# Two transformer blocks on one core: the weights of the layers done by halves lie 64 bytes further in their buffers

## The chip, the cores and the metric

The kernel runs on 1 core of one Trainium2 chip. The metric is the device time of one execution in microseconds (us); less is better. Before the change the median of three runs is 1825.68 us (1824.88 to 1826.26).

## What is computed

Two blocks, one after the other, on 512 tokens of 1024 features, in float32. Nearly all of the arithmetic is in dense layers `x @ w`. Cut to its layers, the reference is:

```
def first_block(x, ...):
    hn = rms_norm(x, g_mix_pre)
    proj = hn @ w_in                          # 1024 x 8192, in pieces
    br_a = spatial_gating(...) @ w_sgu_out
    br_b = conformer_conv(...) @ w_conv_out
    br_c = multiscale_pool(...) @ w_pool_out
    h = x + rms_norm(merged @ w_out, g_mix_post)
    f_gate, f_up = split(rms_norm(h, g_ffn_pre) @ w_ffn_in)
    h = h + rms_norm((silu(f_gate) * f_up) @ w_ffn_out, g_ffn_post)
    return h + sigmoid(h @ w_ple_gate) * (p @ w_ple)

def second_block(x, ...):
    proj = rmsnorm(x, norm_mix_w) @ w_in      # 1024 x 5640, in pieces
    oa = gated_delta_rule(...)                # 4 heads, chunks of 64
    ob = chunk_band_attention(...)            # 8 heads
    x = x + (gates on oa @ w_branch_a, ob @ w_branch_b) @ w_out
    u = causal_dwconv(rmsnorm(x) @ w_up) + conv_ffn_b
    x = x + (silu(gate) * up) @ w_down
    return rmsnorm(x, norm_final_w)
```

## The kernel before

Features lie on the 128 partitions, tokens run along a row, so an activation is 8 tiles of 128 x 512 and a layer's output block `n` (128 features) is summed in one PSUM bank over the input blocks `k`.

A float32 value is kept as two float32r tiles, `hi` (the value rounded) and `lo` (the rest). `mm3` then makes a product of three matmuls, `hi*hi`, `hi*lo` and `lo*hi`: lines 168, 169 and 170. The weight slice, 128 x 128, is the stationary operand that TensorE loads, and the activation is the moving one. Each matmul has a weight load of its own in the trace (LDWEIGHTS, engine PEld).

`prep` brings one chunk of weights, as a rule 128 x 1024, that is eight such slices: a DMA on SyncE's queue into `raw`, a copy on ScalarE into `whi` (line 113) and a subtraction on VectorE into `wlo` (line 116). Of `whi` and `wlo` there are four buffers each, 4096 bytes a partition. `emit` runs the list of steps in order and prepares chunks two ahead.

Most layers are done by `linear`: all 512 tokens at once, matmuls 512 columns wide. Five places are done by `linear_halves`: the same weights first for tokens 0 to 255, then for tokens 256 to 511, so that what follows can start on the first half. Its matmuls are 256 columns wide. These places are `w_out` (output blocks 4 to 7), `w_ffn_in` (the first two blocks), `w_ffn_out` (the last two), `w_ple_gate` (the first three) and `w_down_2` (the last two). Where `hold` gives other tiles for a chunk (named `fl`, `tl`, `xh`, `xl` by their pools), the weights are split into those and not into `whi` and `wlo`.

Every tile starts at a multiple of `LINE`, 128 bytes:

```
LINE = 128
...
        n = -taken % LINE
        if n:
            pool.tile([P, n // 4], F32, name="fill")
```

A slice of weights is 512 bytes of a partition's row, so every slice starts at such a multiple as well. `gm` holds masks of 128 x 128 for the delta rule; of its ten planes the kernel reads nine, 0 to 8 (`gm[:, 4 + lv]` with `lv` up to 4). The pool that holds it, `p2`, comes after the weight buffers, the activations and the small tiles in memory.

The order of the instructions is set by the code's order and, on VectorE within a short reach, by the recording layer's scheduler.

Of the kernel before, what the change touches and what calls it, by code (L numbers as in the profile page):

```python
# [8 lines left out]
F32 = mybir.dt.float32  # L9
F32R = mybir.dt.float32r  # L10
# [5 lines left out]
P = 128  # L16
T = 512
D = 1024
# [25 lines left out]
def build(tc, d, out):  # L44
# [13 lines left out]
    S = {}  # L58
# [87 lines left out]
            i = c.start // T  # L146
            return self.tiles[i][:, c.start - i * T:c.stop - i * T]

    def prep(src, hold=None):
        n = src.shape[-1]  # L150
        raw = wp.tile([P, D], F32, tag="raw", bufs=2, name="raw")
        nc.sync.dma_start(raw[:, :n], src)
        if hold is not None:
            hi, lo = [], []
            for c0 in range(0, n, T):
                h, l = hold(), hold()
                m = min(n - c0, T)
                split(raw[:, c0:c0 + m], h[:, :m], l[:, :m])
                hi.append(h)
                lo.append(l)  # L160
            return Parts(hi), Parts(lo)
        hi = wp.tile([P, D], F32R, tag="whi", bufs=4, name="whi")
        lo = wp.tile([P, D], F32R, tag="wlo", bufs=4, name="wlo")
        split(raw[:, :n], hi[:, :n], lo[:, :n])
        return hi, lo

# [73 lines left out]
    steps = []  # L240
    bgq = deque()

    def step(fn, chunk=None, bg=2400, hold=None):
        steps.append((chunk, fn, bg, hold))

    def emit():
        chunks = [(c, hold) for c, _, _, hold in steps if c is not None]
        pos = 0
        used = 0
        ready = deque()  # L250
        LA = 2
        for c, fn, bg, _ in steps:
            if c is not None:
                used += 1
                while pos < len(chunks) and pos < used + min(LA, used - 1):
                    ready.append(prep(*chunks[pos]))
                    pos += 1
                fn(*ready.popleft())
            else:
                fn()  # L260
            while bg > 0 and bgq:
                cost, f = bgq.popleft()
                f()
                bg -= cost
        assert not bgq
# [26 lines left out]
    def linear_halves(name, nbs, kb, xs, consume, then=None, hold=None):  # L292

        held = {}
        for hf, c in enumerate(HALVES):
            order = [(n, k) for n in nbs for k in kchunks(kb)]
            if hf:
                order.sort(key=lambda nk: nk[1])
            for n, (k0, k1) in order:
                def body(n=n, k0=k0, k1=k1, c=c):  # L300
                    if k0 == 0:
                        held[n, "ps"] = mmps()
                    ps = held[n, "ps"][:, :T // 2]
                    wh, wl = held[n, k0]
                    for k in range(k0, k1):
                        xh, xl = xs(k)
                        w = slice((k - k0) * P, (k - k0 + 1) * P)
                        mm3(ps, wh[:, w], wl[:, w], xh[:, c], xl[:, c], k == 0, k == kb - 1)
                    if k1 == kb:
                        consume(n, ps, c)  # L310

                if hf == 0:
                    def fn(wh, wl, n=n, k0=k0, body=body):
                        held[n, k0] = (wh, wl)
                        body()

                    step(fn, d[name][n][:, k0 * P:k1 * P], hold=hold and hold(n, k0))
                else:
                    step(body)
            if then is not None:  # L320
                step(lambda c=c: then(c))
# [441 lines left out]
    def to_second():  # L763
        st2.close()
        hp.close()
        open_psum("ps2", {"mm": 2, "g0": 2, "g1": 2, "att": 2})
        PS["aux"] = "g0"
        p = S["p2"] = st3.enter_context(tc.tile_pool(name="p2", bufs=1, reuse_waits="tile"))
        S["gm"] = p.tile([P, 10, P], F32, name="gm")
        nc.scalar.dma_start(S["gm"], d["gm"])  # L770
        S["at"] = [None] * 8
        S["vb"] = [None] * NT
        S["A"] = [pair("A") for _ in range(4)] + [None] * 4
        for ap in sum(S["A"][:4], ()):
            dve.memset(ap[:, :1].bitcast(F32), 0.0)
# [492 lines left out]
def layout(inputs):  # L1268
    import numpy as np

    g = {k: np.asarray(a) for k, a in inputs.items()}
    a = {}
    a["xT"] = np.ascontiguousarray(g["x"][0].T).reshape(NB, P, T)
    a["pT"] = np.ascontiguousarray(g["p"][0, 0].T).reshape(2, P, T)

    w = g["w_in"][0]
    a["w_su"] = _pack(w[:, 0:1024])
    a["w_sv"] = _pack_tm(w[:, 1024:2048])
    a["w_ca"] = _pack(w[:, 2048:3072])
    a["w_cg"] = _pack(w[:, 3072:4096])  # L1280
    a["w_z"] = _pack(w[:, 4096:5120])
    a["w_g0"] = _pack(w[:, 5120:6144])
    a["w_g1"] = _pack(w[:, 6144:7168])
    a["w_g2"] = _pack(w[:, 7168:8192])
    for n in ("w_sgu_out", "w_conv_out", "w_pool_out", "w_out", "w_ffn_in", "w_ffn_out", "w_ple_gate"):
        a[n] = _pack(g[n][0])
    w = _pack(g["w_ple"][0])
    a["w_ple"] = np.ascontiguousarray(w.reshape(2, 4, P, 2 * P).transpose(0, 2, 1, 3).reshape(2, P, 8 * P))
    a["w_pool"] = np.concatenate([_pack(g["w_pool"][0, i]) for i in range(4)], axis=0)
    w = g["w_in_2"][0]  # L1290
    a["w_qkv"] = _pack(w[:, 0:1536])
    a["w_za"] = _pack(w[:, 1536:2048])
    a["w_ba"] = np.ascontiguousarray(
        w[:, 2048:2056].reshape(NB, P, 8).transpose(1, 0, 2)).reshape(1, P, 64)
    a["w_qkb"] = _pack(w[:, 2056:3080])
    a["w_vb"] = _pack_tm(w[:, 3080:3592])
    a["w_gab"] = _pack(w[:, 3592:5640])
    a["w_branch"] = np.concatenate([_pack(g["w_branch_a_2"][0]), _pack(g["w_branch_b_2"][0])], axis=2)
    a["w_out_2"] = _pack(g["w_out_2"][0])
    a["w_up_2"] = _pack(g["w_up_2"][0])  # L1300
    a["w_down_2"] = _pack(g["w_down_2"][0])

    vec = np.zeros((P, NVEC), np.float32)

    def put(name, x):
        o, n = VEC[name]
        vec[:, o:o + n] = x

    for n in ("b_dw", "g_conv_ln", "b_conv_ln", "s_pool", "g_mix_post", "g_ffn_pre", "g_ffn_post",
              "norm_mix_w_2", "gdn_norm_w_2", "norm_ffn_w_2", "conv_ffn_b_2"):  # L1310
        put(n, g[n][0].reshape(-1, P).T)
    put("norm_final_w_2", g["norm_final_w_2"].reshape(-1, P).T)
    put("w_dw", g["w_dw"][0, :, 0, :].reshape(TAPS, NB, P).transpose(2, 1, 0).reshape(P, NB * TAPS))
    put("conv_qkv_w_2", g["conv_qkv_w_2"][0].reshape(4, 12, P).transpose(2, 1, 0).reshape(P, 48))
    put("conv_ffn_w_2", g["conv_ffn_w_2"][0].reshape(3, 44, P).transpose(2, 1, 0).reshape(P, 132))
    put("a_log_2", np.tile(g["a_log_2"][0], 4)[None, :])
    put("dt_bias_2", np.tile(g["dt_bias_2"][0], 4)[None, :])
    put("rec", (1.0 / np.arange(1, 17, dtype=np.float32))[None, :])
    a["vec"] = vec
    a["gin"] = np.ascontiguousarray(g["g_mix_pre"][0].reshape(-1, P).T)  # L1320

    a["wsT"] = np.ascontiguousarray(g["w_sgu_s"][0].transpose(2, 0, 1))
    a["bs"] = np.ascontiguousarray(np.broadcast_to(g["b_sgu_s"][0][None], (P, 8, P)))
    a["gv"] = np.ascontiguousarray(np.broadcast_to(g["g_sgu_v"][0][None], (P, D)))
    a["bv"] = np.ascontiguousarray(np.broadcast_to(g["b_sgu_v"][0][None], (P, D)))

    dist = np.arange(P)[:, None] + 384 - np.arange(T)[None, :]
    a["bias"] = np.ascontiguousarray(g["rel_bias_2"][0][:, np.clip(dist, -128, 128) + 128])
    a["bias"][:, :64, T - 64:] = NEG

    i = np.arange(P)
    gm = np.zeros((P, 10, P), np.float32)
    mid = P // 2 - 1
    gm[:, 0] = (np.where((i[:, None] > mid) & (i[:, None] <= i[None, :]), 1.0, 0.0)
                - np.where((i[:, None] <= mid) & (i[:, None] > i[None, :]), 1.0, 0.0))
    gm[:, 1] = np.where(i[:, None] > i[None, :], 0.0, NEG)
    gm[:, 2] = np.where(i[:, None] <= i[None, :], 0.0, NEG)
    gm[:, 3] = np.where((i[:, None] == i[None, :] + 1) & (i[:, None] % 2 == 1), -1.0, 0.0)
    for lv in range(6):
        m = 2 << lv  # L1340
        bi, bj = i[:, None] // m, i[None, :] // m
        gm[:, 4 + lv] = np.where((bj == bi + 1) & (bj % 2 == 1), 1.0, 0.0)
    a["gm"] = gm
    a["ident"] = np.eye(P, dtype=np.float32)
    return a
# [23 lines left out]
```

## Time and profile before

| | |
|---|---|
| median of three runs | 1825.68 us |
| the profiled execution's own time | 1826.73 us |
| its span, first to last instruction | 1824.9 us |
| granted TensorE clock over the span | 0.997 |
| TensorE busy | 1807.8 us (99%) |
| weight loads busy | 1501.4 us (82%) |
| VectorE busy | 1183.0 us (65%) |
| ScalarE busy | 740.6 us (41%) |

PE is TensorE's matmuls and PEld its weight loads, which overlap the matmuls. Matmul records overlap one another too, so what one matmul costs in a stream is read from start to start, not from its duration. A row of a timeline gives the start, the duration, engine, line, operation, output and inputs, the tile of the array used, and the size; `128*128 128x256` is a full stationary slice with 256 moving columns. PE's clock is 1.00 in all the stretches that are looked at here but for the first microseconds.

### The profile page before, as it was taken

How to read it: one execution, taken by the hardware profiler on the slowest of the kernel's cores; microseconds unless marked ns; L12 is line 12 of the kernel's file. 1: busy time of each engine (PE TensorE's matmuls, PEld its weight loads, DVE VectorE, ACT ScalarE, POOL GpSimd, SP SyncE). 2: the span in 40 equal slices, each digit the busy share in tenths (PEclk: the TensorE clock that was granted, in tenths of full speed). 3: DMA queues.
4: the chain of work that ended last, by engine and by line, in shares of the span. 5: the costliest groups of instructions: out<-in, count | busy, mean ns of one | idle time of the engine just before them, and what ended most of it. 6: DMA issues, size and time to landing. Idle time of an engine off the chain costs nothing.

```text
span 1824.9 us, 22886 instructions
## 1 busy us (share of the span) xinstructions
PE 1807.8 (99%) x8932; PEld 1501.4 (82%) x8932; DVE 1183.0 (65%) x2050; ACT 740.6 (41%) x1217; POOL 0.7 (0%) x5
## 2 busy tenths in 40 slices
PE   9999999999999999999999999999999999999997
PEld 7888888888888888888898787887678888888887
DVE  6999977986448444442276684597636577777333
ACT  5442234325346222322345742664434444444221
POOL 0000000000000000000000000000000000000000
PEclk9999999999999999999999999999999999999999
DMA  5333223332353223233335222222235322233331
GB/s 193 104 105 103 93 77 106 106 104 66 119 173 114 95 93 103 93 89 98 114 112 180 66 68 77 76 66 97 99 121 190 127 94 93 98 99 91 95 97 65
DMA packets 62893, 189.73 MB, mean 104 GB/s; under 512 B 7232, under 2 KB 10432, under 8 KB 62784
## 3 DMA queue, kind: packets, MB, share of 16 engines
q1 hardware_dynamic: 56736, 177.53, 30.2%
q10 hardware_dynamic: 6048, 10.73, 1.8%
q8 instruction: 70, 1.15, 0.3%
q14 instruction: 39, 0.32, 0.1%
HBM read 176.70 MB, written 11.53 MB: 103 GB/s over the span
## 4 chain that ended last, share of the span: by engine, by line
PE 94%; DVE 3%; ACT 1%; DMA 1%; issue 1%; SPq 0%; DVEq 0%; ACTq 0%
PE mm L169 27%; PE mm L168 27%; PE mm L170 27%; PE g L977 1%; PE g L982 1%; PE att L1093 1%; DVE wlo L116 1%; ACT whi L113 1%; PE mm L340 1%; PE mm L341 1%; PE att L170 1%; PE att L168 1%; PE att L169 1%; PE mm L339 1%; PE att L1085 1%
## 5 line engine op out<-in xcount | busy, mean ns | idle before, releaser
L113 ACT ACTIVATE whi<-raw 128x1024 fp32r<-128x1024 f32 (+3 forms) x304 | 312.2, 1027 | 659.1 <-PE mm L169 403.3
L116 DVE TENSOR_TENSOR wlo<-raw,whi 128x1024 fp32r<-128x1024 f32 (+3 forms) x304 | 359.2, 1182 | 200.4 <-ACT whi L113 198.5
L168 PE MATMUL mm<-xh,whi 128*128 128x512 f32 (+1 forms) x1032 | 393.7, 382 | 0.0
L169 PE MATMUL mm<-xl,whi 128*128 128x512 f32 (+1 forms) x1032 | 393.2, 381 | 0.0
L170 PE MATMUL mm<-xh,wlo 128*128 128x512 f32 (+1 forms) x1032 | 393.0, 381 | 0.0
L168 PE MATMUL mm<-th,whi 128*128 128x512 f32 (+1 forms) x976 | 379.7, 389 | 0.4 <-ACT th L113 0.4
L169 PE MATMUL mm<-tl,whi 128*128 128x512 f32 (+1 forms) x976 | 379.3, 389 | 0.3 <-DVE tl L116 0.2
L170 PE MATMUL mm<-th,wlo 128*128 128x512 f32 (+1 forms) x976 | 378.0, 387 | 0.0
L170 PEld LDWEIGHTS mm<-xh,wlo 128*128 128x128 f32 x1032 | 193.9, 188 | 37.2
L168 PEld LDWEIGHTS mm<-xh,whi 128*128 128x128 f32 x1032 | 193.9, 188 | 37.2 <-issue 0.2
L169 PEld LDWEIGHTS mm<-xl,whi 128*128 128x128 f32 x1032 | 194.0, 188 | 36.9 <-issue 0.2
L168 PEld LDWEIGHTS mm<-th,whi 128*128 128x128 f32 x976 | 183.5, 188 | 39.4 <-issue 4.6
L169 PEld LDWEIGHTS mm<-tl,whi 128*128 128x128 f32 x976 | 183.6, 188 | 36.6 <-issue 1.9
L170 PEld LDWEIGHTS mm<-th,wlo 128*128 128x128 f32 x976 | 183.6, 188 | 35.2 <-issue 1.2
L125 DVE SCALAR_TENSOR_TENSOR cv<-hc,vec,cv 128x507 f32<-128x507 f32 (+18 forms) x240 | 172.5, 733 | 4.2 <-ACT cv L462 0.6
L170 PE MATMUL mm<-fh,wlo 128*128 128x512 f32 (+1 forms) x252 | 91.0, 361 | 0.0
L116 DVE TENSOR_TENSOR sg<-mm,R 128x512 f32<-128x512 f32 (+1 forms) x43 | 29.1, 678 | 95.4 <-PE mm L170 95.4
L168 PE MATMUL mm<-fh,whi 128*128 128x512 f32 (+1 forms) x252 | 90.8, 360 | 0.0
L169 PE MATMUL mm<-fl,whi 128*128 128x512 f32 (+1 forms) x236 | 84.6, 358 | 0.0
L116 DVE TENSOR_TENSOR t<-mm,R 128x512 f32<-128x512 f32 x56 | 38.5, 688 | 53.9 <-PE mm L170 52.0
L116 DVE TENSOR_TENSOR t<-mm,sg 128x512 f32<-128x512 f32 (+1 forms) x31 | 20.9, 673 | 62.5 <-PE mm L170 62.5
L168 PEld LDWEIGHTS mm<-fh,whi 128*128 128x128 f32 x252 | 47.6, 189 | 7.2
(381 smaller groups left out, 2044.8 us busy)
## 6 DMA issues: line engine op xcount, KB each, us to landing
raw<-in_w_ffn_in SPq DMA_DIRECT2D x44, 512.0 KB, 3.3
raw<-in_w_up SPq DMA_DIRECT2D x44, 512.0 KB, 3.3
raw<-in_w_g SPq DMA_DIRECT2D x24, 512.0 KB, 3.3
raw<-in_w_out SPq DMA_DIRECT2D x16, 512.0 KB, 3.3
raw<-in_w_ffn_out SPq DMA_DIRECT2D x16, 512.0 KB, 3.5
raw<-in_w_gab SPq DMA_DIRECT2D x16, 512.0 KB, 3.4
raw<-in_w_down SPq DMA_DIRECT2D x16, 512.0 KB, 3.5
raw<-in_w_qkv SPq DMA_DIRECT2D x12, 512.0 KB, 3.5
```

The source lines that it names most:

```text
L113: act.activation(out=o, in_=i, func=AF.Copy, scale=scale)
L116: dve.tensor_tensor(out=o, in0=a, in1=b, op=op)
L125: dve.scalar_tensor_tensor(out=o, in0=a, scalar=s, in1=b, op0=op0, op1=op1)
L168: pe.matmul(ps, wh, xh, start=first, stop=False)
L169: pe.matmul(ps, wh, xl, start=False, stop=False)
L170: pe.matmul(ps, wl, xh, start=False, stop=last)
L339: pe.matmul(ps, xh[:, t], wh[:, c], start=(k == 0), stop=False)
L340: pe.matmul(ps, xh[:, t], wl[:, c], start=False, stop=False)
L341: pe.matmul(ps, xl[:, t], wh[:, c], start=False, stop=(k == kb - 1))
L977: pe.matmul(yp[:, B[b]], A[:, B[b]], Z[:, B[b]], start=True, stop=True)
L982: pe.matmul(zp[:, B[b]], Zt[:, B[b]], Y[:, B[b]], start=True, stop=True)
L1085: pe.transpose(pt[:, c:c + P], z[:, c:c + P], ident)
```

## The change

The weight buffers `whi` and `wlo` become 32 elements (128 bytes) longer, 4224 bytes each. A chunk that `linear_halves` asks for is written and read 16 elements (64 bytes) behind the buffer's start; all other chunks stay at the start. To make room, the plane of `gm` that is never read is dropped (512 bytes a partition). The three functions pass the number on.

```
-    def prep(src, hold=None):
+    def prep(src, hold=None, at=0):
...
-        hi = wp.tile([P, D], F32R, tag="whi", bufs=4, name="whi")
-        lo = wp.tile([P, D], F32R, tag="wlo", bufs=4, name="wlo")
+        hi = wp.tile([P, D + 32], F32R, tag="whi", bufs=4, name="whi")[:, at:]
+        lo = wp.tile([P, D + 32], F32R, tag="wlo", bufs=4, name="wlo")[:, at:]
         split(raw[:, :n], hi[:, :n], lo[:, :n])
...
-    def step(fn, chunk=None, bg=2400, hold=None):
-        steps.append((chunk, fn, bg, hold))
+    def step(fn, chunk=None, bg=2400, hold=None, at=0):
+        steps.append((chunk, fn, bg, (hold, at)))
...
-        chunks = [(c, hold) for c, _, _, hold in steps if c is not None]
+        chunks = [(c, *hold) for c, _, _, hold in steps if c is not None]
...
-                    step(fn, d[name][n][:, k0 * P:k1 * P], hold=hold and hold(n, k0))
+                    step(fn, d[name][n][:, k0 * P:k1 * P], hold=hold and hold(n, k0), at=16)
...
-        S["gm"] = p.tile([P, 10, P], F32, name="gm")
+        S["gm"] = p.tile([P, 9, P], F32, name="gm")
...
-    gm = np.zeros((P, 10, P), np.float32)
+    gm = np.zeros((P, 9, P), np.float32)
...
-    for lv in range(6):
+    for lv in range(5):
```

Because the buffers are longer, the four of a kind now lie 4224 bytes apart and no longer 4096, and all that lies behind them in memory moves up by 1024 bytes; what lies behind `gm` in its pool moves by 512.

On TensorE, ScalarE, SyncE and GpSimd the instructions stand in the same order as before. On VectorE one moves, where the second block begins: there the reciprocal root of the norm (`rs_t`, `rs_y`, ending in `Rtm`) is worked out while the small weight chunk `w_ba` is split (`wlo<-raw,whi 128x64`). Before:

```order
L125 SCALAR_TENSOR_TENSOR rs_t<-rs_t,rs_y 128x4
L120 TENSOR_SCALAR rs_y<-rs_y 128x4
L125 SCALAR_TENSOR_TENSOR rs_t<-rs_t 128x4
L116 TENSOR_TENSOR wlo<-raw,whi 128x64
L125 SCALAR_TENSOR_TENSOR Rtm<-rs_t,rs_y 128x4
L116 TENSOR_TENSOR wlo<-raw,whi 128x1024
```

And on the same engine and at the same place after the change:

```order
L125 SCALAR_TENSOR_TENSOR rs_t<-rs_t,rs_y 128x4
L116 TENSOR_TENSOR wlo<-raw,whi 128x64
L120 TENSOR_SCALAR rs_y<-rs_y 128x4
L125 SCALAR_TENSOR_TENSOR rs_t<-rs_t 128x4
L125 SCALAR_TENSOR_TENSOR Rtm<-rs_t,rs_y 128x4
L116 TENSOR_TENSOR wlo<-raw,whi 128x1024
```

The small split stands two instructions earlier; the instruction that ends the root, `Rtm`, has the same ones ahead of it in both.

## The prediction

> **What bounds the kernel now.** I read the page's head and its chain of work, then the groups with their shapes kept apart, then TensorE's timeline where the shapes change.
>
> ```profile
> span 1824.9 us, 22886 instructions
> ...
> PE 1807.8 (99%) x8932; PEld 1501.4 (82%) x8932; DVE 1183.0 (65%) x2050; ACT 740.6 (41%) x1217; POOL 0.7 (0%) x5
> ...
> PE 94%; DVE 3%; ACT 1%; DMA 1%; issue 1%; SPq 0%; DVEq 0%; ACTq 0%
> ```
>
> TensorE is busy for 99% of the span and makes up 94% of the chain that ended last. So the change counts only if it alters the pace of matmuls. The groups say which matmuls get moved weights (line, engine, tiles, shape, count, then busy us and mean ns):
>
> ```profile
> L168 PE MATMUL mm<-xh,whi 128*128 128x512 f32 x952 | 371.6, 390 | 0.0
> ...
> L168 PE MATMUL mm<-th,whi 128*128 128x512 f32 x928 | 366.1, 395 | 0.4 <-ACT th L113 0.4
> ...
> L168 PE MATMUL mm<-fh,whi 128*128 128x512 f32 x184 | 71.6, 389 | 0.0
> ...
> L168 PE MATMUL mm<-xh,whi 128*128 128x256 f32 x80 | 22.1, 283 | 0.0
> ...
> L168 PE MATMUL mm<-fh,whi 128*128 128x256 f32 x68 | 19.2, 283 | 0.0
> ...
> L168 PE MATMUL mm<-xh,fl 128*128 128x256 f32 x48 | 13.7, 285 | 0.0
> ...
> L168 PE MATMUL mm<-th,whi 128*128 128x256 f32 x48 | 13.6, 286 | 0.0
> ```
>
> Only the layers by halves have 256 columns. With weights in `whi` line 168 has 80 + 68 + 48 = 196 of them, and lines 169 and 170 as many, since `mm3` issues all three: 588 matmuls. Weights held in other tiles (the row with `fl` is one kind) stay where they are. Durations overlap one another, so the pace is read from the starts. Here are the first and the last of eleven 512-wide matmuls, the place where 256 follows 512, and the first and the last of 94 in a stretch by halves:
>
> ```profile
> 1019.75 0.39 PE L170 MATMUL mm<-th,wlo 128*128 128x512 f32 x1
> ...
> 1022.02 0.39 PE L168 MATMUL mm<-th,whi 128*128 128x512 f32 x1
> ...
> 532.62 0.39 PE L170 MATMUL mm<-xh,wlo 128*128 128x512 f32 x1
> 532.85 0.28 PE L168 MATMUL mm<-xh,whi 128*128 128x256 f32 x1
> 532.96 0.28 PE L169 MATMUL mm<-xl,whi 128*128 128x256 f32 x1
> 533.08 0.28 PE L170 MATMUL mm<-xh,wlo 128*128 128x256 f32 x1
> ...
> 571.22 0.28 PE L170 MATMUL mm<-th,wlo 128*128 128x256 f32 x1
> ...
> 582.38 0.28 PE L170 MATMUL mm<-th,wlo 128*128 128x256 f32 x1
> ```
>
> A 512-wide matmul takes 2.27 us / 10 = 227 ns of the stream, a 256-wide one 11.16 us / 93 = 120 ns. The difference, 107 ns for 256 columns, is what 256 columns cost as such. So each matmul, of either width, carries 120 - 107 = 13 ns beside its columns. The 588 take 588 x 120 ns = 70.6 us; no more than that is at stake directly.
>
> The other thing a matmul needs is its weight load. Its pace alone shows where matmuls of one column leave nothing but loads, eight in a row (start, us in all), with the duration of one from that group's view; below it stand the mean durations of loads in the stretch by halves and, from the page, over the kernel:
>
> ```profile
> 987.69 0.97 PEld L205 LDWEIGHTS g<-ones,sq 128*128 128x128 f32 x8 [0.30 <-DVE sq L116]
> ...
> L205 PEld LDWEIGHTS g<-ones,sq x8: 186/192/192, 987.7 to 988.5; 128*128 128x128 f32 x8
> ...
> L170 PEld LDWEIGHTS mm<-th,wlo 128*128 128x128 f32 x32 | 6.1, 192 | 0.0
> ...
> L170 PEld LDWEIGHTS mm<-th,wlo 128*128 128x128 f32 x976 | 183.6, 188 | 35.2 <-issue 1.2
> ```
>
> Seven steps take 0.97 - 0.19 = 0.78 us, 111 ns each. That load is of plain float32, not float32r, but of the same 128 x 128 slice. With 256 columns, 120 ns per matmul leave it some 9 ns of room; with 512 it has 116 ns. The loads by halves last 192 ns in the records, as in the stream that is nothing but loads, and 188 ns over the kernel: by halves the load is near its limit. That is the one place where the address of weights could matter.
>
> **The change, part by part.**
>
> *The start of the weights, 64 bytes further, in 588 loads.* The trace has no full slice that starts off a multiple of 128 bytes. The nearest row is the small layer of line 796: its slices have 16 columns, 64 bytes, and lie one behind the other, so every second one starts 64 bytes off such a multiple. Two matmuls use each slice; the rows are of the first two slices, then the matmul behind the last of 16:
>
> ```profile
> 1006.19 0.40 PE L796 MATMUL g<-th,w 128*16 128x512 f32 x1
> 1006.42 0.40 PE L797 MATMUL g<-tl,w 128*16 128x512 f32 x1
> 1006.66 0.40 PE L796 MATMUL g<-th,w 128*16 128x512 f32 x1
> 1006.89 0.40 PE L797 MATMUL g<-tl,w 128*16 128x512 f32 x1
> 1007.13 0.40 PE L796 MATMUL g<-th,w 128*16 128x512 f32 x1
> ...
> 1009.91 0.40 PE L168 MATMUL mm<-th,whi 128*128 128x512 f32 x1
> ```
>
> The two steps from the aligned slice are 0.23 and 0.24 us, those from the other 0.23 and 0.24; 16 steps average 3.72 / 16 = 0.2325 us. No difference shows, though 512 columns would hide a small one. And the 13 ns beside the columns are the same at both widths, which looks like a fixed price of changing weights rather than something that depends on addresses. So I take 0 ns for each of the 588. Ends for the range: below, the load's own pace, 111 ns (588 x -9 ns = -5.3 us), and at the extreme the columns alone, 107 ns (588 x -13 ns = -7.6 us); above, a load that reads 512 bytes as five pieces of 128 in place of four, 111 x 5/4 = 139 ns, an estimate from the load's row, 588 x 19 ns = +11.2 us. Zero is the value that the nearest row gives.
>
> The Trainium skill, "TensorE: Matmul & The Clock Gate", section "What happens when you issue a matmul", says that TensorE has two independent read ports on SBUF, so that loading the next weights takes no read bandwidth from the running matmul. By that no address can free anything and the sum stays 0. [...]
>
> *Writing the weights at the shifted place.* The split is one copy on ScalarE and one subtraction on VectorE per chunk; VectorE's cost at odd starts shows in the convolution's taps, which write from 4 bytes (511 elements) to 64 bytes (496) behind the start, against a full row that starts on a line:
>
> ```profile
> L116 DVE TENSOR_TENSOR wlo<-raw,whi 128x1024 fp32r<-128x1024 f32 x278 | 339.9, 1223 | 148.1 <-ACT whi L113 146.3
> L113 ACT ACTIVATE whi<-raw 128x1024 fp32r<-128x1024 f32 x278 | 294.7, 1060 | 588.7 <-PE mm L169 342.3 <-issue 156.3 <-PE att L169 14.2
> ...
> L125 DVE SCALAR_TENSOR_TENSOR cv<-hc,vec,cv 128x511 f32<-128x511 f32 x8 | 6.0, 748 | 0.6 <-ACT cv L462 0.6
> L125 DVE SCALAR_TENSOR_TENSOR xl<-h,vec,xh 128x512 fp32r<-128x512 f32 x8 | 6.0, 746 | 0.8 <-ACT xh L113 0.8
> ...
> L125 DVE SCALAR_TENSOR_TENSOR cv<-hc,vec,cv 128x496 f32<-128x496 f32 x8 | 5.9, 733 | 0.2
> ```
>
> 748, 746 and 733 ns follow the number of elements, not the start: 0 for VectorE. ScalarE has no such row; its copy takes 1.06 us while TensorE spends 24 x 120 ns = 2.9 us on a chunk, with the chunks prepared two ahead. Even a copy of twice that time would lie beside that work. Without the cover, its extra 1.06 us on 1 + 2 + 4 + 3 + 3 = 13 moved chunks (the five places in order) would cost 14 us.
>
> *The longer buffers.* Their starts now differ by 4224 bytes, so that the full-width layers read weights in four positions relative to their activations, still on multiples of 128. All 512-wide rows above have one pace at 389 to 395 ns duration, with activations in `xh`, `th` and `fh`; none shows a position that matters. I take 0. Bounds: +-1 ns on each of (952 + 928 + 184) x 3 = 6192 matmuls would be +-6.2 us, and I see nothing that would give it.
>
> *`gm` shorter, and the moved split.* One DMA carries 576 KB instead of 640 (an estimate, nine planes of ten):
>
> ```profile
> gm<-in_gm ACTq DMA_DIRECT2D x1, 640.0 KB, 3.9
> ...
> L838 PE MATMUL g<-gs_g,gm x2: 263/273/283, 1022.6 to 1022.7; 128*128 128x16 f32 x2
> ...
> L770 ACTq DMA_DIRECT2D gm<-in_gm x1: 334/334/334, 988.6 to 988.6; - x1
> ...
> 990.53 0.22 DVE L116 TENSOR_TENSOR wlo<-raw,whi 128x64 fp32r<-128x64 f32 x1
> ```
>
> It lands at 988.6 + 3.9 = 992.5 us and TensorE first reads it at 1022.6: 30 us of cover. The small split on VectorE takes 0.22 us and goes two instructions earlier; `Rtm`, which ends the root, has the same work ahead of it: 0, or at most that 0.22 us either way.
>
> *Sum:* 0 + 0 + 0 + 0. The profiled execution took 1826.73 us, 1.8 more than its span and 1.05 above the median of the runs, 1825.68, so I put the forecast on the median: **1825.7 us**, by itself within 1824.7 to 1826.7, about the spread of the runs.
>
> **The rivals.**
>
> *Faster, the load was disturbed (R1).* By halves load and matmul start together (each next load can begin only when the matmul ahead has taken its weights), and both stream from SBUF. The load's pace is 120 ns there, 111 alone, and the first 256-wide matmul behind a 512-wide one took 0.11 us before the pace settled at 0.12. If 64 bytes keep the two streams out of each other's way, the 588 go to 111 to 113 ns: at 112, 588 x -8 ns = -4.7 us, 1821.0. Against it: 512-wide matmuls carry the same 13 ns, although their loads have all the time they need.
>
> *Faster, all of the 13 ns goes (R2).* Then the columns alone are left: 1825.7 - 7.6 = 1818.1 us. For it speaks only that nothing in the profile explains the 13 ns.
>
> *Slower, the load gets longer (R3).* The place is the load of each of the 588, with 9 ns of room at most. If a slice that begins in mid-line is read in five pieces, a load takes 139 ns, becomes the bound by halves and gives 1825.7 + 11.2 = 1836.9 us. It decides as soon as a load lasts over 120 ns, that is 8% longer than alone; it shows above 126 ns (588 x 6.2 ns = 3.65 us). For it: the 192 ns records. Against it: line 796's slices.
>
> *The stagger of the buffers counts (R4),* either way, up to the 6.2 us above.
>
> *The change misses its matmuls* is not a rival of weight: the rows with `whi` are 588 of the 256-wide ones.
>
> **How the numbers follow.** Forecast, nothing measurable: 0.40. R1: 0.20, most of it just past the mark, and 0.06 for a smaller gain. R2: 0.08. R3: 0.11 for the full price, 0.11 for a load between 120 and 130 ns, at most 588 x 9 ns = 5.3 us. R4: 0.04. 0.2% of the time, 3.65 us, is about what a measurement of this kernel can tell from no change. Faster by more: 0.18 of R1, R2 and half of R4, 0.28. Slower by more: full R3, 0.07 of the partial one, half of R4, 0.20. The rest, 0.52, is the same. The range reaches down to R2, 1818.0, and up to the partial R3, 1831.0; it leaves out the full R3 and some of R4.
>
> **What would show it.** In the changed profile the start-to-start step by halves: 120 ns if I am right, 111 to 113 under R1, 107 under R2, over 120 under R3 with PEld as long as before. The step of 512-wide matmuls stays at 227 ns, unless R4 holds. The step by halves of weights in `fl`, `tl` and the like must stay at 120 in every case; if those change too, the cause is not the weights' start. The forecast is wrong if the two read streams share something, or if a load works in lines of 128 bytes.

## The result and the profile after

The changed kernel takes 1843.16 us (median of four runs, 1842.78 to 1844.9) against 1825.8 us (median of four, 1824.88 to 1826.26) for the kernel before: a ratio of 1.0097, interval 1.0084 to 1.0109, or 17.4 us more. The forecast was no change, and the range ended at 1831.0 us. In the experiments below, one execution of ten of the kernel in which weights and activations move together took 4709 us, and its ratio is formed without it (the other nine: 1824.06 to 1826.61).

The head of the page after, with its chain of work (lines of `mm3` are one higher than before: 169, 170, 171):

```profile
span 1843.1 us, 22886 instructions
...
PE 1827.3 (99%) x8932; PEld 1502.3 (82%) x8932; DVE 1184.0 (64%) x2050; ACT 741.2 (40%) x1217; POOL 0.7 (0%) x5
...
PE 95%; DVE 2%; ACT 1%; DMA 1%; issue 1%; SPq 0%; DVEq 0%; ACTq 0%
```

The span grew by 18.2 us and TensorE's busy time by 19.5, with as many instructions as before. PEld, VectorE and ScalarE grew by 1 us or less. So no wait came in; the matmuls got slower. The groups, with their shapes kept apart, say which ones:

```profile
L169 PE MATMUL mm<-xh,whi 128*128 128x512 f32 x952 | 375.2, 394 | 0.0
...
L169 PE MATMUL mm<-th,whi 128*128 128x512 f32 x928 | 368.1, 397 | 0.0
...
L169 PE MATMUL mm<-fh,whi 128*128 128x512 f32 x184 | 72.2, 392 | 0.0
...
L169 PE MATMUL mm<-xh,whi 128*128 128x256 f32 x80 | 22.0, 279 | 0.0
...
L169 PE MATMUL mm<-fh,whi 128*128 128x256 f32 x68 | 18.9, 278 | 0.0
...
L169 PE MATMUL mm<-xh,fl 128*128 128x256 f32 x48 | 13.7, 284 | 0.0
...
L169 PE MATMUL mm<-th,whi 128*128 128x256 f32 x48 | 13.4, 283 | 0.0
```

The 512-wide groups, whose weights were not meant to move, last 2 to 4 ns longer on average (390 to 394, 395 to 397, 389 to 392). The 256-wide ones with moved weights last 3 to 5 ns less (283 to 279, 283 to 278, 286 to 283). Weights held in `fl` stay within 1 ns. The change did its work by halves, a little to the good, and lost on the layers that it left alone.

A mean of 3 ns is a mean over two kinds. Here are, from TensorE's timeline, two chunks of 24 matmuls each, one behind the other. The first row starts the first chunk, the row at 351.16 the second, the row at 356.75 the chunk after them:

```profile
345.70 0.39 PE L169 MATMUL mm<-th,whi 128*128 128x512 f32 x1
...
346.39 0.39 PE L169 MATMUL mm<-th,whi 128*128 128x512 f32 x1
...
350.70 0.39 PE L170 MATMUL mm<-tl,whi 128*128 128x512 f32 x1
350.93 0.40 PE L171 MATMUL mm<-th,wlo 128*128 128x512 f32 x1
351.16 0.40 PE L169 MATMUL mm<-xh,whi 128*128 128x512 f32 x1
351.40 0.40 PE L170 MATMUL mm<-xl,whi 128*128 128x512 f32 x1
...
356.75 0.39 PE L169 MATMUL mm<-xh,whi 128*128 128x512 f32 x1
```

Inside the first chunk, from 346.39 to 350.70, 19 steps take 4.31 us, 227 ns each, as before. (Its first three steps are slower; the last section comes back to them.) The second chunk takes 5.59 us for 24 steps, 233 ns each. Chunks of these two kinds alternate wherever a layer is done for all tokens at once.

What tells them apart is where their buffer lies. The four buffers of a kind now start 0, 4224, 8448 and 12672 bytes behind the first. An activation tile has 2048 bytes a partition, and slices of weights are 512 bytes. So counted modulo 256 bytes, weights lie at the same place as the activations that they meet in buffers 0 and 2, and 128 bytes further in buffers 1 and 3. Before the change all lay at the same place. I call the distance from activations to weights, modulo 256 bytes, the relative place. From the starts of all matmuls in the trace (nanoseconds from one start to the next, where the matmul's own weights and those loaded beside it lie alike):

| | before | after |
|---|---|---|
| 512-wide, relative place 0 | 227.0 | 227.4 (3006 matmuls) |
| 512-wide, relative place 128 | none | 232.7 (3024 matmuls) |
| 256-wide, moved weights | 119.9 (place 0) | 115.3 (place 64), 116.0 (place 192) |
| 256-wide, weights held elsewhere | 119.9 | 119.9 |

The sum: 3024 x 5.7 ns = +17.2 us; 3006 x 0.4 ns = +1.3 us (nearly all of it the first three matmuls behind a border from place 128 to place 0); the matmuls of lines 340 to 342, which use `whi` as the moving operand, +0.8 us; 588 x -4.2 ns = -2.5 us. That is +16.8 us, against 17.4 measured. The steps across a border, where own and loaded weights lie differently, are in none of these terms: 119 from place 0 to 128 are 5.7 ns longer than the same steps before, 121 the other way 8.4 ns, together +1.7 us. With them the sum is 18.5 us, and the span in these two traces grew by 18.2.

### The profile page after: what moved, and what is told of

Same layout as the page of the kernel before. It is cut to its first block, busy times and chain, and to the rows that moved or that the text cites. A ratio compares the mean times of both kernels' runs of the same rounds, so it can differ in the third digit from the quotient of the medians.

```text
span 1843.1 us, 22886 instructions
## 1 busy us (share of the span) xinstructions
PE 1827.3 (99%) x8932; PEld 1502.3 (82%) x8932; DVE 1184.0 (64%) x2050; ACT 741.2 (40%) x1217; POOL 0.7 (0%) x5
## 4 chain that ended last, share of the span: by engine, by line
PE 95%; DVE 2%; ACT 1%; DMA 1%; issue 1%; SPq 0%; DVEq 0%; ACTq 0%
PE mm L170 28%; PE mm L171 28%; PE mm L169 28%; PE g L978 1%; PE g L983 1%; DMA raw<-in_w_sv 1%; PE att L1094 1%; PE att L171 1%; PE att L169 1%; PE att L170 1%; PE att L1086 1%; PE att L1065 0%; ACT whi L113 0%; PE aux L217 0%; DVE wlo L116 0%
```

## The experiments

My theory after the result: a matmul is slowed by the relative place of its weights, modulo 256 bytes. Rivals: buffers 4224 bytes apart are slow as such, whatever lies where (distance); or the absolute address counts, or something else that moved in memory.

**The longer buffers alone.** The changed kernel, but no chunk starts 64 bytes further:

```
-  step(fn, d[name][n][:, k0 * P:k1 * P], hold=hold and hold(n, k0), at=16)
+  step(fn, d[name][n][:, k0 * P:k1 * P], hold=hold and hold(n, k0), at=0)
```

> The longer buffers and the shorter gm alone; no chunk is shifted. Place theory (the pace depends on where the weights start relative to the activations, modulo 256 bytes): half of the 512-wide matmuls, some 3000, stay 5.7 ns slower each, and the gain by halves is gone: about 1845 us, slower than the changed kernel. Shift theory (the 64 bytes made the loads longer): back at 1826 us.

Measured: 1845.65 us, ratio 1.0109 (1.0095 to 1.0123). From the groups with shapes kept apart:

```profile
L169 PE MATMUL mm<-xh,whi 128*128 128x512 f32 x952 | 375.2, 394 | 0.0
...
L169 PE MATMUL mm<-fh,whi 128*128 128x256 f32 x68 | 19.2, 282 | 0.0
```

The 512-wide row is the same as after the change. The whole loss comes with the longer buffers; the 64 bytes by halves are no part of it. The 512-wide steps are 227.4 and 232.7 ns again, the 256-wide ones 119.7 at place 0 and 118.6 at place 128.

**The places repaired, the distance kept.** The changed kernel, in which chunks of buffers 1 and 3 start another 128 bytes further, so that all full-width layers read at relative place 0. `i` counts the chunks; buffers are handed out in the order 0, 3, 2, 1, with one jump at chunk 183:

```
+        i = chunks_split[0]
+        chunks_split[0] += 1
+        place = (-(i - (i >= 183))) % 4
+        at = at or 32 * (place % 2)
```

> The changed kernel, but in every second buffer a full-width chunk starts 128 bytes in, so that all full-width weights start at the same place modulo 256 as the activations; the chunks by halves keep their 64 bytes. Place theory: 512-wide steps back at 227 ns, 256-wide ones with moved weights at 115 to 116 ns, 588 x -4.2 ns = -2.5 us: 1823.2 us, faster than both. Distance theory (the 4224 bytes from buffer to buffer disturb through the writes next door): stays near 1843 us.

Measured: 1823.65 us, ratio 0.9991 (0.9982 to 1.0000). 512-wide steps are 227.0 ns, 256-wide ones with moved weights 115.2 (place 64) and 115.9 (place 192). The buffers are still 4224 bytes apart, so the distance as such costs nothing, and the rival of the distance falls.

**Weights and activations moved together.** The kernel before, with `gm` of nine planes to make room and 128 bytes put in ahead of the weight buffers:

```
+    wp.tile([P, 32], F32, name="fill")
```

> Buffers as before, 4096 bytes, nothing shifted by halves, but weights, activations and all behind them start 128 bytes further (gm has nine planes). Relative place theory: steps of 227 and 120 ns, 1825.7 us. Absolute place theory (the start of the weights itself, modulo 256): all 6558 full-width matmuls 5.7 ns slower, 1863 us. Distance theory: 1825.7 us.

Measured: 1824.77 us, ratio 0.9997 (0.9987 to 1.0006). The steps are 227.0 and 119.8 ns.

**Activations alone moved.** The same 128 bytes, put in behind the weight buffers and ahead of the activations (all that lies behind these moves with them):

```
+    acts.tile([P, 32], F32, name="fill")
```

> Buffers as before, weights where they were, but the activations and all behind them 128 bytes further (gm has nine planes). Relative place theory: all 512-wide steps at 232.7 ns, 1863 us; the 256-wide matmuls whose weights are held in other tiles, which move along with the activations, stay at 120 ns. Absolute place theory and distance theory: 1825.7 us.

Measured: 1858.81 us, ratio 1.0182 (1.0166 to 1.0197), 33.2 us more than before. Here are the groups of this kernel and then those of the one in which all moved together:

```profile
L169 PE MATMUL mm<-xh,whi 128*128 128x512 f32 x952 | 376.8, 396 | 0.0
...
L169 PE MATMUL mm<-xh,whi 128*128 128x256 f32 x80 | 22.0, 281 | 0.0
...
L169 PE MATMUL mm<-xh,fl 128*128 128x256 f32 x48 | 13.7, 285 | 0.0
```

```profile
L169 PE MATMUL mm<-xh,whi 128*128 128x512 f32 x952 | 371.6, 390 | 0.0
...
L169 PE MATMUL mm<-xh,whi 128*128 128x256 f32 x80 | 22.1, 283 | 0.0
...
L169 PE MATMUL mm<-xh,fl 128*128 128x256 f32 x48 | 13.7, 285 | 0.0
```

With weights left where they were, all the 512-wide matmuls now step at 232.5 ns (5.5 ns on each of 6142 steps is 33.8 us; where `whi` is the moving operand 1.5 us come on top, and 0.7 us by halves and some 2 us in shorter waits go back). With weights moved as well, none does. So it is not the address of the weights, nor that of the activations, but the one against the other. Weights in `fl` move with the activations and keep their pace in both. This pair tells the theory from both of its rivals.

**Other places.** Two kernels give each chunk of every layer a place by its buffer, to tell whether the price grows with the distance from 0 or comes at once. In both, `place` and `i` are worked out as above. The first has the relative places 64, 192, 32 and 160:

```
+        at = (16, 16, 8, 8)[place]
```

> The changed kernel with a place of its own for every weight buffer, for all layers: the weights start 32, 64, 160 or 192 bytes behind the activations' start, modulo 256. Read from the steps of each buffer, not from the time. Smooth theory (the price grows with the distance from the activations' place, up to 5.7 ns at 128 bytes): 512-wide steps of about 228.5 ns at 32, 230 at 64 and 192, 231 at 160; 256-wide ones 115 to 116 at 64 and 192, between that and 119 at 32 and 160; about 1845 us. Step theory (every place but the activations' own costs the full 5.7 ns): 232.7 ns everywhere, about 1861 us.

The second has 96, 224, 16 and 144:

```
+        at = (24, 24, 4, 4)[place]
```

> As in the run before, with the places 16, 96, 144 and 224 bytes behind the activations' start. Smooth theory: 512-wide steps of 227.7 ns at 16, 231 at 96, 232 at 144, 228.5 at 224; 256-wide ones 119 at 16, 116 to 117 at 96 and 224, 118 at 144. Step theory: 232.7 ns at all four.

One execution of each, 1857.77 and 1864.2 us, with 1824.83 for the kernel before beside them; they are read by their steps. From the first kernel's timeline the starts of the chunks at places 192 and 64 and of the chunk behind them, and then from the second kernel's the same for place 16 and its follower:

```profile
713.65 0.39 PE L175 MATMUL mm<-th,whi 128*128 128x512 f32 x1
...
719.14 0.40 PE L175 MATMUL mm<-th,whi 128*128 128x512 f32 x1
...
724.75 0.40 PE L175 MATMUL mm<-th,whi 128*128 128x512 f32 x1
```

```profile
710.52 0.40 PE L175 MATMUL mm<-th,whi 128*128 128x512 f32 x1
...
716.11 0.40 PE L175 MATMUL mm<-th,whi 128*128 128x512 f32 x1
```

24 steps take 5.49 us at 192 (229 ns), 5.61 at 64 (234) and 5.59 at 16 (233). All places, with those of the other runs, as the step in ns:

| relative place | 0 | 16 | 32 | 64 | 96 | 128 | 144 | 160 | 192 | 224 |
|---|---|---|---|---|---|---|---|---|---|---|
| 512-wide | 227.0 | 233.3 | 233.3 | 233.4 | 233.9 | 232.7 | 233.4 | 233.2 | 229.2 | 233.4 |
| 256-wide | 119.9 | 118.5 | 118.3 | 116.4 | 118.1 | 118.6 | 118.6 | 119.9 | 116.6 | 118.0 |

With 512 columns the price comes at once, with 16 bytes as with 128; only 192 pays a third of it. That the price grows with the distance is ruled out. With 256 columns place 0 is the slowest, with 160, and 64 and 192 are the best.

In lines 346 to 348 of the first kernel the roles are swapped: `whi` is the moving operand and the activations are the stationary one. There chunks 64 bytes further step at 229.5 ns (75 steps) and chunks 192 bytes further at 233.0 (70 steps), the reverse of the table. So the place that counts is that of the stationary operand relative to the moving one.

**What the 64 bytes by halves are worth.** The repaired kernel without them, and the repaired kernel once more beside it:

```
-        at = at or 32 * (place % 2)
+        at = 32 * (place % 2)
```

> The longer buffers with every chunk, by halves too, brought to the activations' place modulo 256. Place theory: no step differs from before, 227 and 120 ns, 1825.7 us. If the distance between buffers costs anything by itself, slower than that.

> The repaired kernel once more, beside the run without the shift, so that the shift of the 588 is the only difference between the two: 588 x -4.2 ns = -2.5 us by the steps, 1823.2 us against 1825.7. If what the steps gain is given back later (at the ends of the halves, where TensorE waits for other engines), the two times are equal.

Measured: 1826.26 us, ratio 1.0004 (0.9995 to 1.0013), without; 1824.31 us, ratio 0.9992 (0.9984 to 1.0001), with. The first and the last of 94 matmuls by halves in `w_ffn_in`, from the timeline of the kernel without the 64 bytes, and then of the one with them:

```profile
571.00 0.28 PE L177 MATMUL mm<-th,wlo 128*128 128x256 f32 x1
...
582.15 0.28 PE L177 MATMUL mm<-th,wlo 128*128 128x256 f32 x1
```

```profile
572.47 0.28 PE L177 MATMUL mm<-th,wlo 128*128 128x256 f32 x1
...
579.38 0.28 PE L175 MATMUL mm<-th,whi 128*128 128x256 f32 x1
...
581.54 0.28 PE L176 MATMUL mm<-tl,whi 128*128 128x256 f32 x1
...
583.42 0.28 PE L177 MATMUL mm<-th,wlo 128*128 128x256 f32 x1
```

93 steps take 11.15 us without and 10.95 with (119.9 and 117.7 ns). The second stretch is not of one pace: 61 steps to 579.38 take 6.91 us, 113 ns each, and 16 steps from 581.54 take 1.88 us, 118 ns each. Between them lie four steps of 165 to 224 ns, waits that the first stretch does not have; they take back 0.26 us. Over all the layers by halves the time from their first to their last matmul is 121.2 us without and 119.6 with, so 1.6 us; the medians differ by 1.95 us. Steps alone would give 588 x -4.2 ns = -2.5 us; the rest is lost again, some of it in waits like the four above. So the 64 bytes are a gain of some 2 us, seen in the steps; against the kernel before, the repaired kernel is 1.9 and 1.6 us faster, with intervals that just reach no difference. It is the best version that was run.

## Why the prediction was wrong

**What bounds the kernel** was right: TensorE makes up 95% of the chain after the change too, and the whole result is one of its pace.

**The longer buffers** are the step that failed. It took 0 and bounded it by +-1 ns on each of 6192 matmuls, because "all 512-wide rows above have one pace"; measured are +5.7 ns on half of them, 17.2 us. The rows quoted for it could not show what they were quoted for: in the kernel before, the buffers of weights and the tiles of activations of these layers start whole multiples of 2048 bytes apart and slices lie 512 bytes apart, so that `xh`, `th` and `fh` are three samples of one and the same relative place. A row in which the thing in question never varies bounds nothing. The rival R4, which named this very cause, had a chance of 0.04 and a price that came from the same rows.

A row that did vary stood in the prediction: line 796, whose slices of 16 columns lie 64 bytes apart, at 232.5 ns a step. I compared its steps with one another and saw no difference. Beside the 227 ns of the other layers, which I had quoted as well, they are 5.5 ns long, all of them. The theory does not explain it, though. By the program's addresses its eight slices lie at places 0, 64, 128 and 192, twice over, which by the table above would give 230.6 on average, and the slices at place 0 are slow as well: the two steps of the first one, 0.23 and 0.24 us in the rows of the prediction, are 234 ns each in the trace. That line was not tried by itself, and what slows it stays open.

**The 13 ns beside the columns** were taken for "a fixed price of changing weights rather than something that depends on addresses", since they are the same at both widths. That sameness was no finding: the 107 ns of the columns had been taken as the difference between the two steps, so 120 - 107 and 227 - 2 x 107 come out alike whatever the hardware does. And the runs refute the fixed price, if the columns are kept at 107 and 214 ns: they are 8 to 13 ns with 256 columns and 13 to 20 with 512, by the relative place.

**The start of the weights, 64 bytes further,** took 0 and measured -2.5 us by its steps. R1 had the direction and the place right ("64 bytes keep the two streams out of each other's way") and forecast 111 to 113 ns, -4.7 us; the steps are 115 to 116 on average, a mixture of two paces, 113 and 118 ns. R2's 107 ns and R3's longer loads did not come: the loads by halves, from the view of TensorE's loads in that stretch of the changed kernel, last 188 ns, where they lasted 192 before.

```profile
L171 PEld LDWEIGHTS mm<-th,wlo 128*128 128x128 f32 x32 | 6.0, 188 | 0.0
```

The rule of the Trainium skill that the prediction weighed ("TensorE: Matmul & The Clock Gate", section "What happens when you issue a matmul"), two independent read ports, so that loading weights takes nothing from the running matmul, left the sum at 0. The runs show that the place of one operand against the other does count: 128 bytes cost 5.5 ns on each 512-wide matmul. The measurement decides; whether the two reads are what meets, no run here shows.

**Splitting at the shifted place** was right at 0: VectorE's and ScalarE's busy times differ by 1 us and 0.6 us over the whole span, and the kernel that repairs the places, which splits more chunks off the start than the change does, loses nothing.

**`gm` of nine planes and the moved split** were right at 0 as far as `gm` goes: with nine planes and all else moved together the ratio is 0.9997. The moved split was not tried alone, but VectorE's instructions stand in that same kernel in the order of the changed one, so the split is in this ratio too.

## What to carry to other kernels

Before a buffer is padded, work out where it puts every weight slice relative to the activations that stream past it: here, of ten places tried, only the same place modulo 256 bytes kept the pace of wide matmuls, and a pad of 128 bytes on a rotating buffer cost half of them 2.5%. A row of a profile bounds a cost only if the thing that the change varies also varies among the rows; ask what is alike in all of them. A stream that runs 5 ns a step off its neighbours asks for a reason, even if its own steps are alike.

## What was not expected of the hardware

The start of two operands relative to each other, modulo 256 bytes, sets TensorE's pace: 227.0 ns against 232.5 to 233.9 for a 512-wide float32r matmul with a weight load beside it, at every place tried but 0 and 192 (229.2 ns). Modulo 512 nothing more shows: in the changed kernel the wide steps away from the borders are 226.9 at 0 and 226.8 at 256, 232.5 at 128 and 232.5 at 384. With half the columns the order turns round, 119.9 ns at place 0 and 115.3 at 64.

With 256 columns the place alone does not set the pace. At places 64 and 192 every run that has them shows two paces, 113.4 and 117.8 ns, and the averages of 115 to 117 are mixtures of them. The same matmuls at the same addresses, in `w_ffn_in`, run at 118 ns in the changed kernel (45 steps from 580.12 to 585.42) and at 113 in the last run above. What chooses between the two is not known.

The border between two chunks shows that the weights in the array are not the only ones that count. The last matmul of the well-placed chunk above, from 350.93 to 351.16, has well-placed weights of its own, and beside it the first slice of the misplaced chunk is loaded. It is the first to be slow (0.40 us, where those ahead of it inside the chunk last 0.39; in the kernel with the longer buffers alone such a matmul steps at 232.5 ns). But the weights that are loaded beside a matmul do not settle it either: at the other border the first three matmuls of the well-placed chunk, from 345.70 to 346.39, take 230 ns each, though their own weights and those loaded beside them are well placed. Over 119 such borders in this trace these three steps are 228.9, 231.7 and 230.4 ns long, and then 227.0. That the two streams of reads meet in the memory is a reading that fits, and no run here shows it. Why the slowness lasts three matmuls beyond the border, why 192 costs less, and why 256-wide matmuls like other places than 512-wide ones, all stays open. So does what the 372 matmuls by halves with weights held elsewhere would gain from 64 bytes: that was not tried.
